# A hybrid decoder layer in fp32: norm spreads with padded parts, later last spreads, and three small reorderings

## The chip, the cores and the metric

The kernel runs on one core of one Trainium2 chip. The metric is the time of one execution on the device, in microseconds. Before the change the median of 3 runs is 1130.23 us (1129.2 to 1131.2).

## The reference

One layer of a decoder is applied to 1056 tokens: a prompt of 1024, and 8 sequences of 4 new tokens each (the decode tokens) that continue from stored keys and values. The width is 1024, everything is fp32, and `_rms(x, g)` is `x / sqrt(mean(x*x) + eps) * g` over the features of a token.

```python
h = _rms(x, n_mix_pre)
z = h @ w_in                       # 1024 -> 512 q | 128 k | 128 v | 512 u
a = attention(q, k, v)             # 8 heads of 64, 2 kv heads, 128 keys incl. self, one sink per head
m = pool_mixer(u)                  # trailing means over 2/4/8/16 tokens minus the token,
                                   # a 128x128 map for each of 4 groups, a scale per channel
mix = concat([a, m]) @ w_out
x = x + _rms(mix, n_mix_post)
f = _rms(x, n_ffn_pre)
f = (silu(f @ w_gate) * (f @ w_up)) @ w_down      # 1024 -> 2816 -> 1024
x = x + _rms(f, n_ffn_post)
x = x + sigmoid(x @ w_ple_gate) * (p @ w_ple)     # p: 256 per token, given
```

The outputs are the new `x` of all tokens, the last 128 keys and values and the last 15 pooling inputs of the prompt, and the same three buffers of the decode sequences, moved on by 4 tokens.

## The kernel before, in words

**Layout.** Features lie on the 128 partitions, tokens along the free dimension. The 1056 tokens are cut into 3 groups of `N` = 352 columns; group 2 holds the last prompt tokens and the decode tokens. A weight is cut into 128x128 blocks, so nearly every matmul has the shape 128x128 by 352 columns.

**Products in threes.** An fp32 value is held as two parts of type fp32r, `hi` and `lo = value - hi`, made by ScalarE and VectorE in `split` (lines 164 and 165). `gemm` (line 291) issues three matmuls for each 128x128 block: hi weight by hi operand, hi weight by lo operand, lo weight by hi operand. An operand of a half of the features is a tile of 4 rows (parts) of 352 fp32 values each, one behind the other, so the k-th part starts 1408k bytes behind the first.

**Weights.** They are streamed from HBM by SyncE's queue through 3 raw buffers (`w_load`), split into 8 buffers of hi and lo (`w_split`), in the order of `plan`, a few tiles ahead of their use. For groups 0 and 1 the wide products use a scheme with 7 quarter products in place of 8 (Strassen's): the sums of weight quarters S1 to S4 are made on GpSimd in `w_sums` (line 1007) and then split; the differences of operands T1 to T4 are made on VectorE (`t_sum` for the FFN, `e_sum` for the last stage). Group 2 uses the direct products.

**A norm's factor** comes from `rstd_steps` (line 313). The squares are summed over the 8 feature blocks into `acc` (128 x 352). Three small matmuls, `acc` in three windows of 128 tokens by a column of ones, sum over the partitions and put tokens on the partitions. ScalarE and VectorE form 1/sqrt, split it in hi and lo, and write each half as a diagonal into `dg` (lines 331 to 344; the tile has the halves behind each other). After a `yield`, two matmuls of 352 columns, a matrix of ones by each half of `dg`, spread the factor over all partitions: this is the spread. There are three norms before the attention (one for each group), two for each group on the way into the FFN (`ffn_steps`, whose second is that of the FFN's input), and one for each group on the FFN's output (`ple_steps`).

**Order of the work.** Most of TensorE's order is that of the program (`pinned`). `order` keeps a VectorE instruction in program order as long as `ordered[0]` is set, that is, up to the first eviction of the opening stage. Everything else is placed by the scheduler of the framework.

- *Opening.* Projections of the pooling inputs `u`, then of k, v and q, for three groups; the pooling mixer between them.
- *Attention.* `dscores` and `scores` make the scores of the decode tokens and of one block of 128 prompt tokens, `softmax` follows on the other engines, then the weights are transposed (`dturned`, `turned`) and applied (`dvalues`, `values`). Blocks go in the order 5, 6, 7, 0, 1, 2, 3, 4, each block's scores ahead of the values of the block before. `filler` puts pieces of the output projection between. The decode values (`dvalues`) are 2 + 16 small matmuls.
- *Output projection and norms.* `turn` and `chain` (lines 891 to 906) are a planner: `chain` adds a generator of steps, `turn(n)` advances a clock by n products of 128x128 by 352 and runs each step that is due. A step says how much VectorE work it has (`load`) and how long to wait; its next due time is the VectorE time so far plus load / `share` plus wait. `share` is 0.6 here, 0.45 in the FFN, 0.1 while the FFN's last group-2 steps run, and 0.7 at the end.
- *The walk.* The FFN's 22 chunks of 128 hidden features go by 11 slabs of 2. `WALK` has 5 slabs (`AHEAD`) for group 2 alone, 6 slabs for all groups, then the first 5 for groups 0 and 1. `gate_up` makes the hidden values, `downs` and `down` the second product of the slab before. `last_down` does this for a group's last slab and gathers squares. When group 2's last slab is done, `chain(ple_steps(2), 19)` starts its norm; `ple_steps(0)` and `ple_steps(1)` start behind the last item (lines 1283 and 1286).
- *End.* `ple_out` handles group 2's eight blocks of 128 features of the last stage directly; `embed_early` makes products `p @ w_ple` ahead of need. `ple_first` then does the first two quarter products of blocks 7, 5, 3 and 1, and `ple_rest(a, b)` the rest of the pairs (1, 0), (3, 2), (5, 4), (7, 6) in that order: T4, S2, S3, S1, S4, each by its partner. `ple_end` forms the sigmoid, multiplies, adds and stores.

The steps of `ple_steps` between small products and spread are these, with the planner's numbers:

```python
yield 6, 14                          # in rstd_steps: load 6, wait 14, then the spread
...
chain(ple_steps(2), 19)              # behind group 2's last slab, share 0.1
chain(ple_steps(0), 24)              # behind the last slab of group 0, share 0.7
chain(ple_steps(1), 54)              # behind the last slab of group 1
```

Of the kernel before, what the change touches and what calls it, by code (L numbers as in the profile page):

```python
# [11 lines left out]
F32R = mybir.dt.float32r  # L12
# [4 lines left out]
P = 128  # L17
# [44 lines left out]
def trunk_kernel(  # L62
# [43 lines left out]
    def nm(s):  # L106
        cnt[0] += 1
        return f"{s}{cnt[0]}"
# [200 lines left out]
    def order(ins):  # L309
        if ordered[0]:  # L310
            tc.keep_in_program_order(ins)

    def rstd_steps(acc):

        n = acc.shape[1]
        at = (0, P, n - P)
        sm = bank()
        for i, lo in enumerate(at):  # L320
            mm(sm[:, i : i + 1], acc[:, lo : lo + P], ones[:, 0:1], start=True, stop=True)
        sd = spool.tile([P, TB], F32, tag="sd", name=nm("sd"))
        se.activation(sd, sm[:, :TB], AF.Sqrt, bias=epst, scale=1.0 / D)
        ve.reciprocal(sd, sd)
        hl = spool.tile([P, 2, TB], F32R, tag="hl", name=nm("hl"))
        ve.tensor_copy(hl[:, 0], sd)
        ve.tensor_tensor(hl[:, 1], sd, hl[:, 0].bitcast(F32), op=ALU.subtract)
        dg = spool.tile([P, 2, n], F32R, tag="dg", name=nm("dg"))
        f = hl.bitcast(F32)
        rest = n - 2 * P  # L330
        dg1 = lambda: ve.tensor_tensor(
            dg[:, :, : 2 * P].rearrange("p h (i k) -> p h i k", k=P),
            ident.unsqueeze(1).unsqueeze(1).to_broadcast([P, 2, 2, P]),
            f[:, :, 0:2].unsqueeze(3).to_broadcast([P, 2, 2, P]),
            op=ALU.mult,
        )
        dg2 = lambda: ve.tensor_tensor(
            dg[:, :, 2 * P :],
            ident[:, P - rest :].unsqueeze(1).to_broadcast([P, 2, rest]),
            f[:, :, 2:3].to_broadcast([P, 2, rest]),  # L340
            op=ALU.mult,
        )
        order(dg1())
        order(dg2())
        yield 6, 14
        ps = bank()
        for h in range(2):
            mm(ps[:, :n], ones_r, dg[:, h], start=h == 0, stop=h == 1)
        return ps[:, :n]
# [4 lines left out]
    def sum_halves(sqs, g):  # L354

        a, b = sqs
        order(ve.tensor_tensor(a, a, b, op=ALU.add))
        ve.tensor_tensor(a[:, 0:2, :], a[:, 0:2, :], a[:, 2:4, :], op=ALU.add)
        acc = acc_tile(g)
        ve.tensor_tensor(acc, a[:, 0, :], a[:, 1, :], op=ALU.add)  # L360
        return acc
# [477 lines left out]
    def filler(n):  # L839
        for _ in range(n):  # L840
            if fill:
                f, *at = fill.pop(0)
                f(*at)
# [5 lines left out]
    filler(2)  # L849
    ptd = dturned(td)  # L850
    filler(1)
    od = bank()
    dvalues(ptd, od)
    put(od, SEQ, NDEC * DSEQ)
# [1 line left out]
    ge.tensor_copy(kse[:, :, : WIN - DSEQ], ckt[:, :, DSEQ:])  # L856
    ge.tensor_copy(kse[:, :, WIN - DSEQ :], kT[:, SEQ:].rearrange("p (b t) -> p b t", t=DSEQ))
    for a, b in zip(blocks, blocks[1:] + [None]):
        t2 = None if b is None else scores(b)
        filler(1)  # L860
        parts = turned(a, t)
        filler(1)
        values(a, parts)
        t = t2
# [49 lines left out]
    def ffn_steps(g):  # L914

        r = yield from rstd_steps(acc[g])
        for yh, xh in zip(ys[g], x1[g]):
            ve.tensor_tensor(yh, yh, bc4(r), op=ALU.mult)
            ve.tensor_tensor(xh, xh, yh, op=ALU.add)
            se.activation(yh, xh, AF.Square)  # L920
            yield 20, 0
        yield 0, 13
        acc2 = sum_halves(ys[g], g)
        yield 20, 6
        r = yield from rstd_steps(acc2)
        for h in range(2):
            nc.sync.dma_start(x1d[g][h], x1[g][h])
            for c in range(4):
                k = 4 * h + c
                ve.scalar_tensor_tensor(  # L930
                    ys[g][h][:, c, :], x1[g][h][:, c, :], gn[:, 2, k : k + 1], r, op0=ALU.mult, op1=ALU.mult
                )
            yield 14, 0
            if (g, h) == (1, 0):
                t_sum("T1")
                yield 20, 0
            else:
                op = f_operand(ys[g][h], g)
                yield 10, 0
                if g == 2:  # L940
                    fs[2].append(op)
                else:
                    f7[f"B{h + 1}{g + 1}"] = op
        if g == 1:
            for name in ("T3", "T2", "T4"):
                t_sum(name)
                yield 20, 0
# [185 lines left out]
    def ple_steps(g):  # L1133

        pl = half(g, F32R, "pl")
        pls[g] = pl[:, 0:2, :], pl[:, 2:4, :]
        for k in range(2):
            pr = tmp(NS[g], "pr")
            nc.sync.dma_start(pr, p[:, k, OFF[g] : OFF[g + 1]])
            split(pl[:, k, :], pl[:, 2 + k, :], pr)  # L1140
        x2s[g] = []
        for h in range(2):
            x2[g][h] = half(g, s="x2")
            nc.sync.dma_start(x2[g][h], x1d[g][h])
        r = yield from rstd_steps(acc3[g])
        behind = tc.keep_in_program_order if g == 2 else lambda ins: ins
        for h in range(2):
            yh, xh = os_[g][h], x2[g][h]
            behind(ve.tensor_tensor(yh, yh, bc4(r), op=ALU.mult))  # L1149
            for c in range(4):  # L1150
                k = 4 * h + c
                behind(
                    ve.scalar_tensor_tensor(  # L1153
                        xh[:, c, :], yh[:, c, :], gn[:, 3, k : k + 1], xh[:, c, :], op0=ALU.mult, op1=ALU.add
                    )
                )
                if g == 2 and c % 2:
                    yield 6, 0
            yield 12 if g == 2 else 24, 0
            if g == 2:  # L1160
                x2s[g].append(f_operand(xh, g))
            elif (g, h) != (1, 0):
                e7[f"B{h + 1}{g + 1}"] = f_operand(xh, g)
            yield 10, 0
        if g == 1:
            for name in ("T1", "T2", "T3", "T4"):
                e_sum(name)
                yield 20, 0
# [85 lines left out]
    def ple_rest(a, b):  # L1254
        wp, w, js = W2[a]
        p1 = p1s[0][:, a // 2, :]

        def add(out, x, ps):
            ve.tensor_tensor(out, x, ps, op=ALU.add)  # L1259

        need(wp)
        a22 = need(w)
        p4 = product(a22, e7["T4"])
        s = need(js)
        add(p1, p1, product(s["S2"], e7["T2"]))
        u3 = tmp(N, "u3")
        add(u3, p1, product(s["S3"], e7["T3"]))
        c21 = tmp(N, "c21")
        add(c21, u3, p4)
        ple_end(c21, wp, b, 0)  # L1270
        p5 = product(s["S1"], e7["T1"])
        add(u3, u3, p5)
        add(p1, p1, p5)
        ple_end(u3, wp, b, 1)
        add(p1, p1, product(s["S4"], e7["B22"]))
        ple_end(p1, wp, a, 1)

    hid[:] = new_hid
# [107 lines left out]
```

## Time and profile before

| what | value |
|---|---|
| median of 3 runs | 1130.23 us |
| profiled execution, its own time | 1130.37 us |
| its span, first to last instruction | 1128.6 us |
| mean granted clock of TensorE | 0.997 |
| TensorE matmul, busy | 1105.4 us, 6997 instructions |
| VectorE, busy | 785.1 us |
| ScalarE, busy | 459.3 us |
| GpSimd, busy | 200.7 us |
| read from HBM, written | 90.55 MB, 10.11 MB |

The profile is of one execution. PE is TensorE's matmul, PEld its weight load, DVE VectorE, ACT ScalarE, POOL GpSimd and SP SyncE. `L126` is the line of the helper that issues nearly all matmuls, so they are told apart by the names of their operands: `mh`, `ml` are the mixers' outputs, `hid` the FFN's hidden values, `fh`, `fl` an operand in hi and lo, `wh`, `wl` a weight, `sh`, `sl` a weight sum, `acc` the summed squares, `dg` the diagonals, `c` a constant. A row of a timeline has start, length, engine, line, operation, output and inputs, shapes and a count; "[a <-X]" behind it says that the engine idled for a us before it, and which instruction ended that. A spread shows as `dg,c` x2, the small products of a norm as `c,acc` with twice the count, as an fp32 matmul leaves two records.

### The profile page before, as it was taken

What the parts mean: (1) busy time and instruction counts of PE and PEld (TensorE: products, weight loads), DVE (VectorE), ACT (ScalarE), POOL (GpSimd) and SP (SyncE); (2) the same over time, 40 slices, a digit from 0 to 9 for tenths busy, and PEclk for the clock granted to TensorE, in tenths of its full rate; (3) what the DMA queues carried; (4) which work ended last, traced back from release to release, by engine and by line L of the source; (5) the groups of instructions that cost most, each with busy time, mean ns of one, the idle gap of its engine ahead of it and who ended that gap; (6) DMA issues with size and microseconds to landing.
All of it is one profiled execution on the core that took longest, in us unless ns stands there. A gap on an engine that the chain in (4) does not pass through costs nothing.

```text
span 1128.6 us, 17518 instructions
## 1 busy us (share of the span) xinstructions
PE 1105.4 (98%) x6997; PEld 1085.6 (96%) x6997; DVE 785.1 (70%) x1296; ACT 459.3 (41%) x823; POOL 200.7 (18%) x169
## 2 busy tenths in 40 slices
PE   8999999999999999999999999999999999999986
PEld 8999978899999999999999999999999999999986
DVE  6766368876979955355465555548887877789887
ACT  8322367665645433331222213123424334356442
POOL 0044022100000221021111102111141132100242
PEclk9999999999999999999999999999999999999999
DMA  8121310442643212021120202113212212246141
GB/s 286 57 69 42 111 50 23 178 178 89 219 137 133 87 45 87 19 75 38 38 76 12 82 20 75 38 38 119 82 53 94 71 61 94 94 145 216 62 151 64
DMA packets 35986, 101.79 MB, mean 90 GB/s; under 512 B 4260, under 2 KB 14916, under 8 KB 35904
## 3 DMA queue, kind: packets, MB, share of 16 engines
q1 hardware_dynamic: 34576, 98.90, 25.8%
q10 hardware_dynamic: 1328, 1.77, 0.5%
q8 instruction: 55, 0.90, 0.3%
q14 instruction: 27, 0.22, 0.1%
HBM read 90.55 MB, written 10.11 MB: 89 GB/s over the span
## 4 chain that ended last, share of the span: by engine, by line
PE 87%; DVE 4%; ACT 3%; issue 2%; POOL 1%; DMA 1%; POOLq 0%; ACTq 0%; SPq 0%; DVEq 0%
PE b L126 87%; POOL wr L1007 1%; DMA xr<-in_x_dram 1%; PE b L120 1%; ACT h L392 1%; ACT wh L164 0%; DVE sg L1220 0%; DVE yo L1222 0%; DVE o L1130 0%; ACT sh L164 0%; ACT a L662 0%; DMA c<-in_gains_dram 0%; DVE o L1149 0%; DMA wr<-in_w_in_dram 0%; DVE x L1153 0%
## 5 line engine op out<-in xcount | busy, mean ns | idle before, releaser
L126 PE MATMUL b<-hid,wh 128*128 128x352 f32 x1056 | 254.3, 322 | 2.6 <-DVE o L1149 2.1
L164 ACT CAST wh<-wr 128x1024 fp32r<-128x1024 f32 (+1 forms) x135 | 138.6, 1029 | 255.0 <-PE b L126 203.3
L126 PE MATMUL b<-fh,wh 128*128 128x352 f32 x712 | 230.1, 323 | 0.0
L126 PE MATMUL b<-fh,wl 128*128 128x352 f32 x712 | 230.0, 323 | 0.0
L126 PE MATMUL b<-fl,wh 128*128 128x352 f32 x712 | 228.6, 321 | 0.0
L1007 POOL TENSOR_TENSOR wr<-wr 128x512 f32<-128x512 f32 x52 | 72.0, 1385 | 744.8 <-DVE wl L165 459.0
L165 DVE TENSOR_TENSOR wl<-wr,wh 128x1024 fp32r<-128x1024 f32 (+1 forms) x135 | 165.4, 1228 | 45.2 <-ACT wh L164 44.7
L126 PEld LDWEIGHTS b<-hid,wh 128*128 128x128 f32 x1056 | 184.6, 188 | 3.3 <-issue 2.4
L126 PE MATMUL b<-hid,wl 128*128 128x352 f32 x528 | 170.4, 323 | 0.0
L126 PE MATMUL b<-fh,sl 128*128 128x352 f32 x416 | 134.6, 324 | 4.8 <-DVE sl L165 4.8
L1104 DVE TENSOR_TENSOR o<-o,b 128x352 f32<-128x352 f32 x240 | 115.1, 515 | 30.5 <-PE b L126 30.2
L126 PE MATMUL b<-fh,sh 128*128 128x352 f32 x416 | 134.7, 324 | 0.5 <-DVE p L1259 0.5
L126 PEld LDWEIGHTS b<-fl,wh 128*128 128x128 f32 x712 | 134.9, 189 | 0.0
L126 PE MATMUL b<-fl,sh 128*128 128x352 f32 x416 | 133.5, 321 | 0.0
L126 PEld LDWEIGHTS b<-fh,wl 128*128 128x128 f32 x712 | 133.4, 187 | 0.0
L126 PEld LDWEIGHTS b<-fh,wh 128*128 128x128 f32 x712 | 133.4, 187 | 0.0
L165 DVE TENSOR_TENSOR sl<-wr,sh 128x1024 fp32r<-128x1024 f32 x52 | 63.6, 1222 | 82.0 <-ACT sh L164 82.0
L164 ACT CAST sh<-wr 128x1024 fp32r<-128x1024 f32 x52 | 53.9, 1047 | 145.3 <-POOL wr L1007 102.3
L126 PE MATMUL b<-h,wh 128*128 128x352 f32 x480 | 104.8, 323 | 1.2 <-ACT h L392 1.0
L126 PEld LDWEIGHTS b<-hid,wl 128*128 128x128 f32 x528 | 98.9, 187 | 0.0
L126 PEld LDWEIGHTS b<-fh,sl 128*128 128x128 f32 x416 | 77.9, 187 | 6.3 <-DVE sl L165 6.3
L126 PEld LDWEIGHTS b<-h,wh 128*128 128x128 f32 x480 | 81.5, 188 | 2.3 <-ACT h L392 1.3
(186 smaller groups left out, 1690.4 us busy)
## 6 DMA issues: line engine op xcount, KB each, us to landing
wr<-in_w_gu_dram SPq DMA_DIRECT2D x64, 512.0 KB, 3.3
wr<-in_w_dn_dram SPq DMA_DIRECT2D x32, 512.0 KB, 3.6
wr<-in_w_pg_dram SPq DMA_DIRECT2D x18, 512.0 KB, 3.5
x<-in_x_dram SPq DMA_DIRECT2D x6, 704.0 KB, 9.2
x1d<-x SPq DMA_DIRECT2D x6, 704.0 KB, 3.5
x<-x1d SPq DMA_DIRECT2D x6, 704.0 KB, 6.8
out_y_dram<-yo SPq DMA_DIRECT2D x24, 176.0 KB, 1.8
wr<-in_w_out_b_dram SPq DMA_DIRECT2D x8, 512.0 KB, 3.5
```

What stands on the lines that cost most here:

```text
L120: ins = te.transpose(out, src, ident)
L126: ins = te.matmul(*args, **kw)
L164: fix(se.copy(hi, src))
L165: fix(ve.tensor_tensor(lo, src, hi.bitcast(F32), op=ALU.subtract))
L392: fix(se.activation(hi[:, c, :], t[:, c, :], AF.Identity, scale=gc))
L1007: ge.tensor_tensor(out, a, b, op=op)
L1104: ve.tensor_tensor(o, o, v, op=ALU.add)
```

## The change

1. *Padding.* `dg` is allocated with 384 columns per half and used up to 352, so that the second half starts 1536 instead of 1408 bytes behind the first. This is so for every norm.
2. *Even small products.* With `even` set, `rstd_steps` issues a fourth small product, a repetition of the third into a column that nobody reads. `even` is set for the norm of the FFN's input of group 1 alone, the last norm in the program before those of `ple_steps`.
3. *Last spreads.* The wait between small products and spread becomes an argument; it is 28 instead of 14 for the three norms in `ple_steps`.
4. *Decode values.* In the attention, the scores of block 6 are issued ahead of the decode values and no longer behind them.
5. *S4.* In `ple_rest`, the product of S4 and B22 is issued behind that of S2 and T2, for all pairs but the last, and its sum goes onto p1 behind the S3 product; before, it was the last of the pair.
6. *First add of squares.* `sum_halves` keeps its first add in program order only for group 1. As `order` works only in the opening stage, and group 2's is made after that, this concerns group 0's first add in the opening.

```diff
-    def rstd_steps(acc):
+    def rstd_steps(acc, wait=14, even=False):
         n = acc.shape[1]
         at = (0, P, n - P)
         sm = bank()
-        for i, lo in enumerate(at):
+        for i, lo in enumerate(at + at[2:] * even):
             mm(sm[:, i : i + 1], acc[:, lo : lo + P], ones[:, 0:1], start=True, stop=True)
...
-        dg = spool.tile([P, 2, n], F32R, tag="dg", name=nm("dg"))
+        dg = spool.tile([P, 2, 3 * P], F32R, tag="dg", name=nm("dg"))[:, :, :n]
...
-        yield 6, 14
+        yield 6, wait
         ps = bank()
...
     def sum_halves(sqs, g):
         a, b = sqs
-        order(ve.tensor_tensor(a, a, b, op=ALU.add))
+        add = ve.tensor_tensor(a, a, b, op=ALU.add)
+        if g == 1:
+            order(add)
...
     filler(1)
+    t2 = scores(blocks[1])
     od = bank()
     dvalues(ptd, od)
...
     for a, b in zip(blocks, blocks[1:] + [None]):
-        t2 = None if b is None else scores(b)
+        t2 = None if b is None else t2 if a == blocks[0] else scores(b)
...
-        r = yield from rstd_steps(acc2)
+        r = yield from rstd_steps(acc2, even=g == 1)
...
-        r = yield from rstd_steps(acc3[g])
+        r = yield from rstd_steps(acc3[g], 28)
...
         add(p1, p1, product(s["S2"], e7["T2"]))
+        early_s4 = b < KC - 2
+        if early_s4:
+            s4 = product(s["S4"], e7["B22"])
         u3 = tmp(N, "u3")
         add(u3, p1, product(s["S3"], e7["T3"]))
+        if early_s4:
+            add(p1, p1, s4)
         c21 = tmp(N, "c21")
...
         ple_end(u3, wp, b, 1)
-        add(p1, p1, product(s["S4"], e7["B22"]))
+        if not early_s4:
+            add(p1, p1, product(s["S4"], e7["B22"]))
         ple_end(p1, wp, a, 1)
```

## The prediction

> **What bounds the kernel now.** I read the page first, then the timeline of TensorE for its idle stretches, then counts in long windows.
>
> ```profile
> span 1128.6 us, 17518 instructions
> PE 1105.4 (98%) x6997; PEld 1085.6 (96%) x6997; DVE 785.1 (70%) x1296; ACT 459.3 (41%) x823; POOL 200.7 (18%) x169
> ```
>
> TensorE is the bound almost everywhere, so two things can move the end: its idle stretches, and the time from one matmul's start to the next. For the second I put two stretches without idle time beside each other; the columns are window, length, TensorE's busy time and instructions, then the other engines, the granted clock, the DMA share and GB/s.
>
> ```profile
> 400.00:790.00 390.00, 390.00 (x2422) 390.00 (x2421) 214.63 (x357) 109.25 (x169) 63.94 (x48) 1.00 0.17 55
> 882.00:1002.00 120.00, 120.00 (x757) 120.00 (x756) 92.34 (x147) 48.63 (x69) 27.61 (x20) 1.00 0.28 90
> ```
>
> Both are full of the same 128x128 by 352 products at full clock. A matmul takes 0.32, so those that reach over an edge add 0.32 to the stretch: 390.32/2422 = 161.1 ns each in the walk, 120.32/757 = 158.9 ns later. The same product has two paces, 2.2 ns apart. Where they change shows in the timeline of TensorE (start, length, operation): `c,acc` are the small products of a norm, `dg,c` its spread of two parts.
>
> ```profile
> 228.02 0.41 PE L126 MATMUL b<-mh,wh 128*128 128x352 f32 x1
> 231.97 0.51 PE L126 MATMUL b<-dg,c 128*128 128x352 f32 x2
> 232.32 0.32 PE L126 MATMUL b<-mh,wh 128*128 128x352 f32 x1
> ...
> 257.11 0.72 PE L126 MATMUL b<-c,acc 128*128 128x1 f32 x6
> 257.69 0.41 PE L126 MATMUL b<-mh,wh 128*128 128x352 f32 x1
> ...
> 261.59 0.49 PE L126 MATMUL b<-dg,c 128*128 128x352 f32 x2
> 261.92 0.32 PE L126 MATMUL b<-mh,wh 128*128 128x352 f32 x1
> ...
> 277.38 1.39 PE L126 MATMUL b<-c,acc 128*128 128x1 f32 x12
> 278.64 0.41 PE L126 MATMUL b<-fh,wh 128*128 128x352 f32 x1
> ...
> 347.75 0.49 PE L126 MATMUL b<-dg,c 128*128 128x352 f32 x2
> ...
> 795.64 0.72 PE L126 MATMUL b<-c,acc 128*128 128x1 f32 x6
> 796.22 0.41 PE L126 MATMUL b<-fh,sh 128*128 128x352 f32 x1
> ...
> 809.66 0.49 PE L126 MATMUL b<-dg,c 128*128 128x352 f32 x2
> ```
>
> By the code 24 products lie between 228.02 and 231.97 (less the first one's 0.08: 161 ns), 156 between 232.32 and 257.11 (158.9), 24 between 257.69 and 261.59 (159.0), 96 between 261.92 and 277.38 (161.0), 84 between 796.22 and 809.66 (159.0). So the pace is a state: it lasts for as long as products come in their usual threes, and it flips at a spread (232 to fast, 261.6 and 809.7 to slow) or at small products (795.6 to fast; 257 leaves it fast, 277 slow). After 347.75 nothing but threes comes until 795.6: whatever pace the last spread leaves holds for the whole walk, and it left the slow one.
>
> **The change part by part**, against this execution's 1130.37 (span 1128.6 and 1.8 around it); the runs' median, 1130.23, is the same to 0.01%.
>
> **Pace: padded parts, four small products.** A row of 352 values is 1408 bytes, so the k-th part of any operand starts at 1408k: the even parts on a multiple of 256, the odd ones halfway. The usual threes alternate three even, three odd; the spread is one even, one odd. Padded to 384 (1536 bytes), it is two even. The trace has no such spread. Its price lies between no effect and a whole fast walk: 795.64 less 347.75 and the spread is 447.5 us, 2778 products at 161.1; at 158.9 they take 6.1 us less. Taking the spread for ordinary products, and for each next start the one that the trace has after the nearest position of the starts with the same parities, I get what happened for one even and one odd part (slow) and, for two even ones, mostly the fast pace out of a slow one and a middle pace (about 160 ns, half the gain, 3.1) out of a fast one. That is an estimate, with little to hold it beyond two steps. I take -6.1. The fourth product changes which pace meets the last spread: six more small records took (278.64 - 277.38) - (257.69 - 257.11) = 0.68, so two more cost +0.2. All later norms have padded spreads too: the 120 us stretch above, and all of 825 to 1003 us, is fast now and could turn slow: 178/0.159 = 1120 products, +2.5 at most; I take 0, as the walk meets it differently anyhow.
> The Trainium skill (TensorE: Matmul & The Clock Gate, "Back-to-back issue gap") has the time from start to start depend on the number of columns alone, some 149 ns for 352. By it neither padding nor a fourth product could change the pace, and this term would be 0; the two windows above, the same shape at one clock, speak against it, but none shows what padding does.
>
> **Decode values behind block 6's scores.**
>
> ```profile
> 136.30 2.12 PE L126 MATMUL b<-a,a 64*128 64x32 f32 x20
> 138.35 0.43 PE L126 MATMUL b<-mh,wh 128*128 128x352 f32 x1
> ...
> 144.48 0.32 PE L126 MATMUL b<-mh,wl 128*128 128x352 f32 x1
> 146.90 4.91 PE L126 MATMUL b<-a,a 32*64 32x128 f32 x52 [2.10 <-ACT y L802]
> 151.74 0.57 PE L126 MATMUL b<-mh,wh 128*128 128x352 f32 x1
> ```
> ```profile
> 146.35 0.41 DVE L777 COPY a<-b 32x256 f32<-32x256 f32 x1
> ```
> ```profile
> 145.00:148.60 3.60, 1.70 (x38) 1.53 (x40) 0.82 (x4) 2.02 (x10) 2.66 (x3) 1.00 0.10 40
> 148.60:152.00 3.40, 3.40 (x17) 2.33 (x15) 1.06 (x3) 0.91 (x4) 0.53 (x2) 0.51 0.38 154
> ```
>
> TensorE could go on at 144.64 (144.48 + 0.16) and waits to 146.90. The page names a copy on ACT; VectorE's copy of the turned decode weights ends at the same time (146.76), and these products read it. Then come 36 records of decode values and 16 of block 6's scores; the clock falls to 0.51 from 148.6, and the scores run at half speed. At full clock 20 records with block 5's scores took 2.05 (136.30 to 138.35). With the scores first: 144.64 + 2.0 = 146.6, a rest of 0.3 to 146.9 for the copy, decode values as before (52 records end at 151.74; the 36 at about 148.3, since the scores start the slow stretch), next product at 148.3 instead of 151.74, and that product's own 0.25 of slow clock is gone too: -3.7. Scores and values issue no DMA; block 6's copies and softmax get onto ACT and VectorE earlier, ahead of the values' copies. Bounds: -3.9, and -2.0 if the clock still falls (it would then halve 3.4 us of full products).
> The Trainium skill (the same page, "What's actually happening") has the clock fall after an idle window of about 3.4 us. The wait here was 2.3, and the waits of 2.1 below cost no clock: by this rule the wait is not the cause, the many small products may be, and they stay.
>
> **Last spreads 14 products on.** By the code's own reckoning (each step is due a load divided by a share after the last, plus the wait, at the next turn), group 2's spread moves from 84 to 96 products behind its small ones, and its VectorE steps with it.
>
> ```profile
> 824.76 0.43 PE L126 MATMUL b<-hid,wh 128*128 128x352 f32 x1 [0.44 <-DVE hid L165]
> ...
> 873.38 0.56 PE L126 MATMUL b<-hid,wh 128*128 128x352 f32 x2 [2.11 <-DVE o L1149]
> ```
> ```profile
> 870.48 1.23 DVE L165 TENSOR_TENSOR sl<-wr,sh 128x1024 fp32r<-128x1024 f32 x1 [3.73 <-ACT sh L164]
> 871.62 1.61 DVE L1149 TENSOR_TENSOR o<-o,b 128x1408 f32<-128x1408 f32 x1
> ```
>
> TensorE stands 2.1 us for a bank while VectorE does a split and the norm's multiply (L1149), which stand ahead of the evictions. Two products' groups later the multiply stands behind some of them. Both waits gone: -2.6; the 1.6 us multiply met elsewhere: up to +1.6. I take -1.1, about half the larger wait, as the split stays where it is.
>
> Group 0's spread:
>
> ```profile
> 1007.50 0.32 PE L126 MATMUL b<-hid,wl 128*128 128x352 f32 x1
> 1009.92 0.58 PE L126 MATMUL b<-dg,c 128*128 128x352 f32 x2 [2.10 <-DVE dg L337]
> ```
> ```profile
> 1003.00:1066.00 63.00, 60.90 (x383) 60.61 (x382) 59.92 (x83) 38.06 (x53) 1.54 (x2) 1.00 0.43 148
> ```
>
> By the same reckoning it moves 30 products on (due 36.6 behind its small ones, next turn at 54 instead of 24), past 1012.4; its operand is there by 1009.9, so the 2.3 us wait is gone. But VectorE is busy 59.92 of 63 us here, and the end game hangs on it:
>
> ```profile
> 1063.48 0.68 DVE L165 TENSOR_TENSOR w<-wr,w 128x512 fp32r<-128x512 f32 x1
> ```
> ```profile
> 1064.38 1.30 POOL L1007 TENSOR_TENSOR wr<-wr 128x512 f32<-128x512 f32 x1 [90.11 <-DVE w L165]
> ...
> 1088.58 1.30 POOL L1007 TENSOR_TENSOR wr<-wr 128x512 f32<-128x512 f32 x1 [5.89 <-DVE w L165]
> ...
> 1101.48 1.51 POOL L1007 TENSOR_TENSOR wr<-wr 128x512 f32<-128x512 f32 x1 [7.02 <-DVE w L165]
> ```
>
> POOL's sums of the last weights start when VectorE has split a tile (1063.48), and then go round every 12 to 13 us with a load, a split and the next sum, whatever TensorE does. So of the 2.3 us only what lets VectorE reach 1063.48 sooner survives. Group 1's spread stays at its turn, the differences T1 to T4 come 36 products later in the program, behind that split rather than ahead of it: up to two steps of 1.6 us earlier for POOL, or idle VectorE time for want of work. I take -1.2, bounds -3.2 and +5.8 (36 products of 161 ns).
>
> **S4 moved.**
>
> ```profile
> 1087.95 0.43 PE L126 MATMUL b<-fh,sl 128*128 128x352 f32 x1 [0.66 <-DVE sl L165]
> ...
> 1100.83 0.43 PE L126 MATMUL b<-fh,sl 128*128 128x352 f32 x1 [1.77 <-DVE sl L165]
> ```
>
> S3 waits for the second split in pairs (3, 2) and (5, 4); S4 needs only the first, and its 12 products (1.9 us) fill both waits, 2.4 together. But TensorE then arrives that much earlier at the next pair's first split, which hangs on POOL's round above. No DMA moves: p1's output still leaves last. I take -0.3, bounds -2.4 and 0.
>
> **Start.** Group 0's first add of squares loses its place in VectorE's order; VectorE's queue decides a single wait:
>
> ```profile
> PE b L126 <- DVE acc L360: 1.0, 1, 1.0
> ```
>
> 0, bounds 0 and +0.6 (one more operation ahead of it, as long as one eviction).
>
> Sum: -6.1 + 0.2 - 3.7 - 1.1 - 1.2 - 0.3 = -12.2; 1130.4 - 12.2 = 1118.2.
>
> **The rivals.**
> *Middle pace.* The last spread is met in the fast state and leaves 160 ns: -3.1 instead of -6.1, 1121.2. For it: the same estimate gives this for half the possible entries. Against: the fourth product shifts the entry.
> *The pace stays.* The state flips for another reason than the parts' places, or padding doesn't reach it: the walk at 161.1, 1124.3. For it: 277 left the pace slow with twelve small records. Against: 261.6 and 809.7, where an even and an odd part ended a fast stretch twice alike.
> *The clock still falls* behind the decode values: 1118.2 + 1.7 = 1119.9. For it: waits of 2.1 at 873 and 1009.9 kept full clock, so idleness alone isn't it. Against: block 5's scores with decode scores at 134 to 138 kept it too.
> *Late spreads starve the end (slower).* VectorE, with nothing to do until group 0's spread lands 30 products later, brings T1 to T4 and POOL's first sum 5.8 us later, and group 2's multiply stands in front of another wait (+1.6). With a walk that stays slow that is -3.7 + 0.2 + 1.6 + 5.8 = +3.9: 1134.3. It decides once the delay of the end exceeds the 3.5 that the decode part saves. For it: 59.92 of 63 leaves no slack. Against: VectorE has 60 us of other work there.
>
> **How the numbers follow.** Forecast 0.50, middle pace 0.21, pace stays 0.15, clock falls 0.07, starved end 0.07. A measurement here tells 0.2% (2.3 us) from no change. Faster: all of the first, second and fourth, and two thirds of the third; the rest of it and a little of the last are within: 0.88 / 0.07 / 0.05. Without the unlikely ends the forecast's own range is 1115 to 1121. It reaches up over the middle and the unchanged pace, 1126, and down to 1113.5, where the waits at 824 and 873 go altogether and POOL starts two steps earlier.
>
> **What would show it.** Right: a window inside the walk at 158.9 ns a product; no TensorE idle time near 145 and clock 1.00 to 152; block 6's scores ahead of the decode values; no wait for `dg` behind the last walk item; POOL's first sum no later than 1064.4 less what was gained before. Wrong: 161 ns in the walk, a stretch at 161 between 825 and 1003, a new wait for `fh` or `fl` at T4's product, or longer waits for the first split of each pair in place of the second.

## The result, and the profile after

The changed kernel takes 1119.11 us (median of 4 runs, 1117.57 to 1120.09), the kernel before in the same session 1129.72; the ratio is 0.9906 (95% interval 0.9886 to 0.9925). Run again later on another occasion, the same kernel gave 1117.87 us and 0.9883 (0.9868 to 0.9898) against 1131.45. The profiled execution is at 1118.45, its span at 1116.7. The forecast was 1118.2.

The page of the changed kernel begins so:

```profile
span 1116.7 us, 17519 instructions
...
PE 1098.3 (98%) x6999; PEld 1080.0 (97%) x6999; DVE 778.4 (70%) x1296; ACT 458.8 (41%) x823; POOL 201.2 (18%) x169
```

The span is 11.9 us shorter. To see where, I put the start of the same 352-column product in the two profiles side by side (counted from the first product; the products of the spreads are left out of the count):

| product | before | after | difference | gained since the row above |
|---|---|---|---|---|
| 96, behind the opening's first 96 products | 24.25 | 23.79 | -0.46 | -0.5 |
| 800, behind the decode values | 153.27 | 149.31 | -3.96 | -3.5 |
| 1800, early in the walk | 352.91 | 348.35 | -4.56 | -0.6 |
| 4535, last item but one ahead of 795 us | 793.55 | 782.91 | -10.64 | -6.1 |
| 4735, behind the first wait at group 2's spread | 827.41 | 817.99 | -9.42 | +1.2 |
| 5010, behind the second | 873.38 | 862.12 | -11.26 | -1.8 |
| 5735, ahead of group 0's spread | 988.66 | 979.11 | -9.55 | +1.7 |
| 5850, behind it | 1010.34 | 998.32 | -12.02 | -2.5 |
| 6200, start of the last stage's pairs | 1067.49 | 1055.47 | -12.02 | 0.0 |
| the last | 1121.76 | 1109.44 | -12.32 | -0.3 |

**The walk.** Windows of the changed kernel (window, length, TensorE's busy time and instructions, the other engines, granted clock, DMA share, GB/s):

```profile
258.00:273.00 15.00, 15.00 (x97) 15.00 (x96) 13.65 (x18) 9.54 (x14) 0.00 (x0) 1.00 0.35 111
400.00:790.00 390.00, 390.00 (x2458) 390.00 (x2458) 216.26 (x362) 111.89 (x172) 68.38 (x52) 1.00 0.17 54
906.00:1002.00 96.00, 96.00 (x599) 96.00 (x598) 75.08 (x131) 41.55 (x62) 16.75 (x12) 1.00 0.33 109
```

In the same 390 us of the walk there are 2458 products, not 2422: 390.32/2458 = 158.8 ns each. The clock is 1.00 in both. From 906 to 1002 us it is the other way round: 96.32/599 = 160.8, where the kernel before had 158.9. The timeline of TensorE shows where the pace of the walk is set:

```profile
257.56 0.48 PE L126 MATMUL b<-dg,c 128*128 128x352 f32 x2
...
333.68 0.94 PE L126 MATMUL b<-c,acc 128*128 128x1 f32 x8
...
343.27 0.48 PE L126 MATMUL b<-dg,c 128*128 128x352 f32 x2
...
784.98 0.72 PE L126 MATMUL b<-c,acc 128*128 128x1 f32 x6
...
800.91 0.48 PE L126 MATMUL b<-dg,c 128*128 128x352 f32 x2
```

The spread at 343.27 is the last before 784.98, as the one at 347.75 was. It was met in the slow pace in both kernels: the 52 products between its small products and it go at 161.2 ns. The spread at 257.56 was met in the fast pace, and the products behind it keep that pace: 97 in the 15 us, where 161 ns would show 95 or 96. In the kernel before the pace turned slow at this spread.

**The decode values.** TensorE's timeline and windows:

```profile
144.25 2.00 PE L126 MATMUL b<-a,a 64*128 64x256 f32 x16
146.50 1.48 PE L126 MATMUL b<-a,a 32*64 32x128 f32 x36 [0.25 <-ACT y L804]
```
```profile
145.00:148.60 3.60, 3.35 (x52) 2.71 (x49) 2.41 (x8) 2.79 (x12) 2.77 (x4) 1.00 0.08 32
148.60:152.00 3.40, 3.40 (x26) 3.38 (x25) 2.75 (x11) 2.48 (x14) 0.13 (x1) 1.00 0.01 2
```

The scores now fill the wait (2.00 us at full clock, a rest of 0.25), and the clock does not fall.

**The last spreads.** TensorE no longer stands for `dg` at group 0's spread. Of the two waits near group 2's spread, the second is nearly gone and the first has grown; a third has come:

```profile
814.93 1.00 PE L126 MATMUL b<-hid,wh 128*128 128x352 f32 x2 [1.62 <-ACT hid L164]
...
862.12 0.59 PE L126 MATMUL b<-hid,wh 128*128 128x352 f32 x2 [0.27 <-DVE o L1107]
...
905.70 0.59 PE L126 MATMUL b<-hid,wh 128*128 128x352 f32 x2 [0.28 <-DVE o L1107]
...
1003.15 0.48 PE L126 MATMUL b<-dg,c 128*128 128x352 f32 x2
```

The first waits for ScalarE's cast of a hidden value. ScalarE's timeline, the kernel before first and then the changed one:

```profile
820.14 0.49 ACT L164 CAST hid<-u 128x352 fp32r<-128x352 f32 x1 [1.72 <-DVE u L1085]
824.35 1.05 ACT L164 CAST sh<-wr 128x1024 fp32r<-128x1024 f32 x1 [3.73 <-POOL wr L1007]
```
```profile
813.45 1.04 ACT L164 CAST sh<-wr 128x1024 fp32r<-128x1024 f32 x1 [3.68 <-POOL wr L1010]
814.40 0.48 ACT L164 CAST hid<-u 128x352 fp32r<-128x352 f32 x1
```

The two casts have changed places: the hidden value now stands behind the cast of a weight sum, which waits 3.68 us for GpSimd.

**The end.** GpSimd's first sum of the first, second and last of its four last rounds, and TensorE's waits for the splits in the pairs:

```profile
1053.39 1.29 POOL L1010 TENSOR_TENSOR wr<-wr 128x512 f32<-128x512 f32 x1 [88.92 <-DVE w L165]
...
1065.53 1.55 POOL L1010 TENSOR_TENSOR wr<-wr 128x512 f32<-128x512 f32 x1 [5.46 <-DMA wr<-in_w_pg_dram]
...
1089.62 1.51 POOL L1010 TENSOR_TENSOR wr<-wr 128x512 f32<-128x512 f32 x1 [5.86 <-DVE w L165]
```
```profile
1074.09 0.43 PE L126 MATMUL b<-fh,sl 128*128 128x352 f32 x1 [0.67 <-DVE sl L165]
...
1084.89 0.43 PE L126 MATMUL b<-fh,sh 128*128 128x352 f32 x1 [1.31 <-ACT sh L164]
...
1086.98 0.43 PE L126 MATMUL b<-fh,sl 128*128 128x352 f32 x1 [1.51 <-DVE sl L165]
```

GpSimd starts 10.99 us earlier than before (1064.38), about a microsecond less than TensorE had gained by product 6200, and TensorE has a new wait of 0.89 in front of the first weight sum (at 1062.88). From the first round's start to the fourth's it is 36.23 us, where it was 37.10. The two waits at 1084.89 and 1086.98 are for the two halves, `sh` and `sl`, of one tile's split, the first of the pair.

### The profile page after: what moved, and what is told of

Read it like the earlier page. It is cut to its first block, busy times and chain, and to the rows that moved or that the text cites. A ratio compares the mean times of both kernels' runs of the same rounds, so it can differ in the third digit from the quotient of the medians.

```text
span 1116.7 us, 17519 instructions
## 1 busy us (share of the span) xinstructions
PE 1098.3 (98%) x6999; PEld 1080.0 (97%) x6999; DVE 778.4 (70%) x1296; ACT 458.8 (41%) x823; POOL 201.2 (18%) x169
## 4 chain that ended last, share of the span: by engine, by line
PE 82%; DVE 6%; POOL 3%; ACT 3%; issue 2%; DMA 2%; ACTq 0%; SPq 0%; POOLq 0%; DVEq 0%
PE b L126 81%; POOL wr L1010 3%; DVE wl L165 1%; DVE sl L165 1%; ACT sh L164 1%; DMA xr<-in_x_dram 1%; PE b L120 1%; DVE o L1133 1%; ACT h L394 1%; DVE sg L1223 1%; DVE yo L1225 1%; DMA wr<-in_w_pg_dram 0%; ACT wh L164 0%; DMA wr<-in_w_gu_dram 0%; ACT a L664 0%
## 5 line engine op out<-in xcount | busy, mean ns | idle before, releaser
L1010 POOL TENSOR_TENSOR wr<-wr 128x512 f32<-128x512 f32 x52 | 75.0, 1442 | 736.1 <-DVE wl L165 453.4
L126 PEld LDWEIGHTS b<-fh,sh 128*128 128x128 f32 x416 | 78.0, 188 | 4.8 <-ACT sh L164 2.0
```

What stands on the lines that cost most here:

```text
L126: ins = te.matmul(*args, **kw)
L1010: ge.tensor_tensor(out, a, b, op=op)
```

## The experiments

Times stand against the kernel before in the same session, whose median was 1131.4 to 1131.7 us in all of them; the changed kernel had two sessions of its own (1119.11 and 1117.87), so single microseconds are read from the profiles.

### What sets the pace of the walk

**The distance of the halves**, in the changed kernel:

```diff
-        dg = spool.tile([P, 2, 3 * P], F32R, tag="dg", name=nm("dg"))[:, :, :n]
+        dg = spool.tile([P, 2, 416], F32R, tag="dg", name=nm("dg"))[:, :, :n]
```

> The changed kernel with one number altered: a half of dg takes 416 columns and not 384, so the second half starts 1664 bytes behind the first, which is again halfway between multiples of 256, as the 1408 of the kernel before. Theory of the place (the spread flips the pace by whether its second part stands at an even or an odd multiple of 128 bytes): the spread behind the four small products leaves the slow pace, the walk goes at 161 ns a product, 6.1 us longer, and the time is about 1125 us (1124 to 1126.5). Rival, padding as such (any shift of the tiles in memory, or the fourth small product, or the earlier entry into the walk, sets the pace): the walk stays at 158.9 ns and the time at 1119 us.

1125.68 us (ratio 0.9952, 0.9938 to 0.9966). The walk of this kernel:

```profile
400.00:790.00 390.00, 390.00 (x2423) 390.00 (x2422) 213.46 (x354) 109.15 (x169) 64.00 (x48) 1.00 0.16 54
```

390.32/2423 = 161.1 ns. More padding, and the gain of the walk is gone: padding as such falls, the place of the second half decides.

**Both halves at odd places**, in the changed kernel:

```diff
-... name=nm("dg"))[:, :, :n]
+... name=nm("dg"))[:, :, 32 : 32 + n]
```

> The changed kernel with dg's columns 32 to 383 used in place of 0 to 351: both halves then start at odd multiples of 128 bytes, where the changed kernel has both at even ones and the kernel before one of each. Theory of like places (only halves of unlike places leave the slow pace): the walk is not at 161 ns, but at 158.9 (1119.1) or, as the replay of the old trace's starts has it, at 160 (1122.2). Rival (a multiple of 256 for both is what counts): the walk at 161 ns, 1125.2.

1119.64 us (0.9893, 0.9862 to 0.9925), and the walk is fast:

```profile
400.00:790.00 390.00, 390.00 (x2458) 390.00 (x2457) 216.23 (x362) 111.82 (x172) 67.66 (x51) 1.00 0.17 55
```

So a multiple of 256 is not what counts for the walk: at the last spread two halves at like places leave the fast pace, two at unlike places the slow one. Places are counted from the start of the tile, whose own address no profile shows. The middle pace, which the replay of the old starts gave, did not come in the walk.

**Three small products in place of four**, in the changed kernel:

```diff
-        r = yield from rstd_steps(acc2, even=g == 1)
+        r = yield from rstd_steps(acc2)
```

> The changed kernel with three small products in place of four ahead of group 1's last spread in front of the walk. Theory A (the padded spread alone sets the pace, since the three small products leave the slow pace here as those at 322 us did): the walk stays at 158.9 ns, 1119 us less 0.2. Theory B (three small products leave the fast pace, and a padded spread met in it leaves the middle one): the walk at 160 ns, 3.1 us longer, 1122 us. Theory C (the number of small records decides): the walk at 161 ns, 6.1 longer, 1125 us.

1118.6 us (0.9888, 0.9857 to 0.992), and 2458 products in the 390 us once more:

```profile
400.00:790.00 390.00, 390.00 (x2458) 390.00 (x2458) 216.26 (x362) 111.82 (x172) 67.95 (x51) 1.00 0.16 54
```

Theory A. The other side of it is **the fourth small product alone**, in the kernel before:

```diff
-        for i, lo in enumerate(at):
+        for i, lo in enumerate(at + at[2:] * even):
...
-        r = yield from rstd_steps(acc2)
+        r = yield from rstd_steps(acc2, even=g == 1)
```

> The kernel before with the fourth small product ahead of group 1's last spread and nothing else, dg at 352 columns. Theory of the places (a spread of unlike halves leaves the slow pace, however it is met): the walk stays at 161 ns a product, 1130 us. Rival (the fourth product shifts the entry so that the spread leaves another pace): the walk at 158.9 or 160 ns, 1124 or 1127 us.

1132.38 us (one run):

```profile
400.00:790.00 390.00, 390.00 (x2423) 390.00 (x2422) 215.16 (x359) 109.37 (x170) 63.96 (x48) 1.00 0.16 54
```

The walk stays slow. The fourth product neither is needed nor does anything by itself.

**Padding alone**, in the kernel before:

```diff
-        dg = spool.tile([P, 2, n], F32R, tag="dg", name=nm("dg"))
+        dg = spool.tile([P, 2, 3 * P], F32R, tag="dg", name=nm("dg"))[:, :, :n]
```

> The kernel before with nothing but the padding of dg to 384 columns. Theory A (padding alone sets the pace): the walk at 158.9 ns, 6.1 us less than before, some 1123.7 us; with the middle pace, 3.1 less, 1126.7. Theory C (the fourth small product is needed): the walk stays at 161 ns and the time within 1 us of the kernel before, 1129.7. If the pace behind 825 us turns slow, up to 2.5 us come on top.

1125.23 us (0.9948, 0.9928 to 0.9967), 6.2 less than before, with a fast walk in the profiled execution:

```profile
400.00:790.00 390.00, 390.00 (x2458) 390.00 (x2457) 217.17 (x363) 112.55 (x173) 64.93 (x49) 1.00 0.17 56
```

Its ten runs lie between 1121.4 and 1128.4, wider than those of the changed kernel, and the profiled one is among the shortest (1122.04); what the longer ones did was not seen.

**How far the rule of like places goes.** In all 14 profiles it holds at the last spread ahead of the walk, which was met in the slow pace each time, at the spread near 258 us, at group 2's near 800 and at the very last one. It does not hold everywhere. Behind the spread near 228 us, with the halves at like places, the changed kernel's first profile, its second one and the run with three small products show this:

```profile
229.00:252.00 23.00, 23.00 (x147) 23.00 (x146) 17.18 (x23) 12.84 (x22) 0.00 (x0) 1.00 0.30 109
229.00:252.00 23.00, 23.00 (x145) 23.00 (x144) 17.03 (x23) 12.66 (x22) 0.00 (x0) 1.00 0.29 109
229.00:252.00 23.00, 23.00 (x146) 23.00 (x145) 17.66 (x24) 13.13 (x22) 0.00 (x0) 1.00 0.29 110
```

By the starts these are 158.9, 161.1 and 160.0 ns: the first two come from one program, and the third is the middle pace, which exists. Two spreads back to back near 283 us leave 161.1 ns in every profile but that of both halves at odd places, which has 158.9. What sets these is open.

### The decode values

```diff
     filler(1)
+    t2 = scores(blocks[1])
     od = bank()
     dvalues(ptd, od)
...
-        t2 = None if b is None else scores(b)
+        t2 = None if b is None else t2 if a == blocks[0] else scores(b)
```

> The kernel before with block 6's scores ahead of the decode values and nothing else. Theory: TensorE's wait of 2.26 us at 144.6 us goes and the clock stays at 1.00 up to 152 us; 3.5 us less than before, 1126.2 us (1125.5 to 1127), and all later paces as before, the walk at 161 ns. Rival (the clock falls behind the decode values all the same): 2.0 less, 1127.7. Rival (the gain is lost later, because the attention waits for softmax): within 1 us of 1129.7.

1127.28 us (0.9968, 0.9953 to 0.9984). TensorE's timeline of this kernel has the same two rows as the changed one:

```profile
144.68 2.00 PE L126 MATMUL b<-a,a 64*128 64x256 f32 x16
146.94 1.48 PE L126 MATMUL b<-a,a 32*64 32x128 f32 x36 [0.26 <-ACT y L802]
```

A ratio of 0.9968 is 3.6 us (1.8 to 5.3 by its interval), in line with the 3.5 of the table: the gain is kept to the end, and the walk stays slow here (2423 products in the 390 us).

### The last spreads

**Group 2 at 14 again**, in the changed kernel:

```diff
-        r = yield from rstd_steps(acc3[g], 28)
+        r = yield from rstd_steps(acc3[g], 14 if g == 2 else 28)
```

> The changed kernel with the wait of 14 back for group 2's spread (28 stays for groups 0 and 1). Theory of the exchange (the later spread only moved the multiply of L1152 from one wait to another): the wait behind the walk's end, 1.9 us for the hi part of hid, shrinks to 0.6, the one some 46 us later grows from 0.3 to 2.1, and the time is within 0.7 us of the changed kernel's 1119.1; if the stretch behind it, now at 161 ns a product for 98 us, turns fast, up to 1.8 less. Rival (the prediction's term of -1.1 for the later spread is right): 1.1 longer, 1120.2.

1117.37 us (0.9877, 0.9847 to 0.9908). Both waits are back, at 0.57 and 1.58 where the kernel before had 0.44 and 2.11:

```profile
814.39 0.43 PE L126 MATMUL b<-hid,wh 128*128 128x352 f32 x1 [0.57 <-DVE hid L165]
...
862.48 0.56 PE L126 MATMUL b<-hid,wh 128*128 128x352 f32 x2 [1.58 <-DVE o L1152]
```

0.57 + 1.58 = 2.15 with the earlier spread, 1.62 + 0.27 + 0.28 = 2.17 with the later: an exchange. The forecast's -1.1 for this step falls. The five other profiles with 14 beside the kernel before have 1.3 to 1.8 in the two waits together, so the 2.11 was a long one; the seven with 28 have 1.8 to 2.2. In two of the seven the clock fell behind the first wait as well (0.73 from 820 to 826 us in the run with 416 columns, 0.66 from 815 to 820 with three small products).

**Group 0 at 14 again**, in the changed kernel:

```diff
-        r = yield from rstd_steps(acc3[g], 28)
+        r = yield from rstd_steps(acc3[g], 14 if g == 0 else 28)
```

> The changed kernel with the wait of 14 back for group 0's spread alone. In any case TensorE waits some 2.3 us for dg again behind the walk's last item. Theory A (POOL's rounds carry half of it to the end, as forecast): 1.2 us longer, 1120.3. Theory B (the whole wait reaches the end): 2.3 to 2.6 longer, 1121.6. Theory C (POOL's first sum is as early as before, so nothing reaches the end): 1119.1.

1121.5 us (0.9917, 0.9889 to 0.9944), 2.4 to 3.6 above the changed kernel. TensorE's wait, a window behind it, and GpSimd's first sum of the end:

```profile
1000.03 0.65 PE L126 MATMUL b<-dg,c 128*128 128x352 f32 x2 [2.10 <-DVE dg L337]
```
```profile
1000.40:1004.00 3.60, 3.60 (x15) 3.60 (x14) 3.60 (x7) 0.95 (x2) 0.00 (x0) 0.53 0.00 0
```
```profile
1055.77 1.29 POOL L1010 TENSOR_TENSOR wr<-wr 128x512 f32<-128x512 f32 x1 [91.40 <-DVE w L165]
```

By its number this is Theory B, but part of it is the clock. It fell behind the wait (0.53 for 3.6 us), which it had not done behind the same wait in the kernel before:

```profile
1010.00:1014.00 4.00, 4.00 (x25) 4.00 (x26) 4.00 (x7) 0.95 (x2) 0.00 (x0) 1.00 0.00 0
```

Counted from product 5735, which precedes the wait, product 5880 starts 28.04 us later here, 26.49 in the kernel before and 24.36 in the changed one: 2.1 for the wait, 1.55 for the clock. GpSimd's first sum starts 77.01 behind product 5735 here (1055.77 - 978.76), 75.72 in the kernel before and 74.28 in the changed one. Padding alone and the four small products alone, at full clock, have 75.46 and 75.81; scores first, with the clock at 0.53 behind the wait, has 77.29. So at full clock the earlier spread costs GpSimd's first sum 1.2 to 1.5 us, near the forecast's half, while TensorE loses the whole wait. The fourth sum is later by all of it again: 112.82 behind product 5735 in the kernel before, 110.51 in the changed one. Why the rounds between are longer with the earlier spread was not looked into.

### S4 moved

```diff
-        early_s4 = b < KC - 2
+        early_s4 = False
```

> The changed kernel with S4's product back at the end of every pair. Forecast: 0.3 us longer, 1119.4, because the waits of the next pair's first split grow by what those of the second shrink. Rival (the 12 products fill waits that nothing takes back): up to 2.4 longer, 1121.5.

1118.18 us (0.9882, 0.9852 to 0.9912). TensorE's waits in the pairs of this kernel:

```profile
1075.01 0.43 PE L126 MATMUL b<-fh,sl 128*128 128x352 f32 x1 [0.67 <-DVE sl L165]
...
1085.53 0.43 PE L126 MATMUL b<-fh,sh 128*128 128x352 f32 x1 [0.93 <-ACT sh L164]
...
1086.79 0.43 PE L126 MATMUL b<-fh,sl 128*128 128x352 f32 x1 [0.67 <-DVE sl L165]
1089.35 0.43 PE L126 MATMUL b<-fh,sl 128*128 128x352 f32 x1 [0.38 <-DVE sl L165]
```

Neither expectation: it is no longer. These four waits are 2.65, the three of the changed kernel 3.49. The wait for `sh` is there with S4 last too (0.93); moving S4 took the 0.38 of the second split and made the two waits for the first split longer, 1.31 + 1.51 in place of 0.93 + 0.67. The times alone (1118.18 against 1119.11 and 1117.87) do not tell, but the starts do: from product 6200 to the last it takes 53.4 to 55.0 us in the six profiles with S4 moved and 28 for group 0, and 53.1 and 53.3 in the two with S4 last (this one and the one with both steps undone). In three of the six the clock fell behind these waits (0.50 to 0.73 for 6 us), in the two it did not.

### The changed kernel again, and two versions beside it

**The same kernel** (no edit):

> The changed kernel once more, beside the next ones on one chip, so that differences of a microsecond can be read. Expected: the walk at 158.9 ns a product as in its first profile, 1119 us (1117.5 to 1120.5), and, if the slow stretch from 905 to 1003 us hangs on a wait of 0.45 us, that stretch again at 161 ns.

1117.87 us. Its windows:

```profile
906.00:1002.00 96.00, 96.00 (x606) 95.85 (x605) 76.20 (x132) 41.55 (x62) 16.64 (x12) 1.00 0.33 109
...
1086.00:1092.00 6.00, 6.00 (x21) 6.00 (x22) 5.86 (x11) 0.57 (x2) 3.24 (x3) 0.50 0.48 147
```

The walk is as before (2459 products in the 390 us). The slow stretch from 906 to 1002 us is not: 96.32/606 = 158.9. So the pace in that stretch differs between executions of one program, as it does behind the spread near 228 us, while the last spread left the same pace in both. The wait of 0.28 in front of the stretch is 0.15 here by the starts; but two other runs (three small products, group 0 at 14) have 0.25 there and stay at the fast pace. And here the clock fell to 0.50 from 1086 to 1092 us, where the first profile of this kernel has 1.00.

**Group 2 at 14 and S4 last together:**

> The changed kernel with group 2's spread at 14 again and S4's product at the end of each pair again; padding, four small products, scores first and 28 for groups 0 and 1 stay. If the two undone steps cost 1.7 and 0 to 0.9 us, as their own runs suggest: 1116.5 us, 1 to 3 us below the changed kernel. Rival (those differences were scatter): within 0.7 us of it.

1116.64 us (0.9868, 0.9852 to 0.9885), 1.2 below the changed kernel in the same session, with overlapping intervals. Undoing the two steps costs nothing; that it gains is likely and not settled by the times.

**Two of the four sums on VectorE in the last stage**, in that kernel (`i` numbers the four sums from 0):

```diff
-            ge.tensor_tensor(out, a, b, op=op)
+            (ve if tail[0] and i in (1, 3) else ge).tensor_tensor(out, a, b, op=op)
...
     early = {}
+    tail[0] = True
```

> The kernel with group 2's spread at 14 and S4 last, and in the last stage the second and fourth of the four weight sums on VectorE and not on GpSimd. If GpSimd's rounds bound the end, each round is some 2.4 us shorter, TensorE's waits in the last pairs (6.5 us in the changed kernel) shrink by 2 to 5 us, and the time is 1112 to 1114.5 us. Rival (VectorE, busy most of that time, is the bound, and its two more operations of some 0.6 us each stand in front of splits and evictions): the waits stay or grow, 1116 to 1119 us.

1112.91 us (0.9845, 0.9822 to 0.9867), the shortest of all; its four runs lie between 1111.52 and 1117.16, and the profiled one is the shortest. GpSimd's first sum of the first and the last round with the last round's second one, and TensorE's waits in the pairs:

```profile
1051.63 1.30 POOL L1012 TENSOR_TENSOR wr<-wr 128x512 f32<-128x512 f32 x1 [88.47 <-DVE w L165]
...
1085.27 1.50 POOL L1012 TENSOR_TENSOR wr<-wr 128x512 f32<-128x512 f32 x1 [5.18 <-DVE w L165]
...
1089.57 1.51 POOL L1012 TENSOR_TENSOR wr<-wr,wr 128x512 f32<-128x512 f32 x1 [2.79 <-DVE wr L1012]
```
```profile
1070.42 0.43 PE L126 MATMUL b<-fh,sl 128*128 128x352 f32 x1 [0.35 <-DVE sl L165]
...
1082.25 0.50 PE L126 MATMUL b<-fh,sh 128*128 128x352 f32 x1 [2.28 <-ACT sh L164]
1083.51 0.66 PE L126 MATMUL b<-fh,sl 128*128 128x352 f32 x1 [0.46 <-DVE sl L165]
```

From the first round's start to the fourth's it takes 33.64 us, and 1088.66 - 1052.96 = 35.70 in the kernel without this edit. The rounds are shorter by 0.7 each and not by 2.4, since GpSimd's second sum now waits up to 2.79 us for VectorE to do its own. Against the kernel without this edit, beside it, the median is 3.7 less and the span of the profile 5.7 (1109.7 against 1115.4). By the starts of the same products 1.3 of the 5.7 are there before the last stage (1023.25 against 1021.92 us; 0.5 of them from product 96 on, so not from the edit), 1.8 come in the last stage (the last product starts at 1108.30 against 1105.19), and 2.6 behind the last product. There VectorE begins seven operations after the last product's start without this edit and two with it. So GpSimd's rounds bound a part of the end; why VectorE is less behind, with two operations more to do in each round, was not looked into.

## Why the prediction was right, step by step

The time and the way were right: -12.2 forecast, -11.9 in the span. The terms, one by one:

- **Pace of the walk, -6.1: right.** The table has -6.1, and the distance of 416 columns takes the gain away again. The pace as a state that the last spread leaves, and the halves' places as what flips it there, both held. The estimate behind it was half right. For a spread of two even parts met in the slow pace it gave mostly the fast one, and so it came: the last spread was met in the slow pace in all 14 profiles. For one met in the fast pace it gave the middle one; at 257.56 it leaves the fast one. The condition of the rival of the middle pace, a last spread met in the fast state, never arose, with three small products or four; the rival of a pace that stays falls by the count. The prediction called this an estimate with little to hold it, and there is some luck in it: behind the spread near 228 us halves at like places do not leave the fast pace each time.
- **Fourth small product, +0.2.** The count of its records is as forecast (8 against 6, 0.22 us longer); as a means to shift the entry it does nothing for the walk, with padding or without (the latter in one run).
- **The Trainium skill's rule** (TensorE: Matmul & The Clock Gate, "Back-to-back issue gap"), by which the columns alone set the spacing and this term would be 0: the runs decide against it, with 161.1 and 158.8 ns for the same shape at clock 1.00, and a layout that switches between them. The 149 ns are worked out from the section's formula for an isolated matmul, of which it says that it gives too much for a stream at many columns; here it gives too little.
- **Decode values, -3.7: right** (-3.5), with the rest of 0.25 forecast as 0.3, and the clock kept. The rival of the falling clock falls here.
- **Group 2's spread, -1.1: wrong.** The second wait went as argued, from 2.11 to 0.27, as the multiply now stands behind the evictions. What failed is "Both waits gone": the first one grew from 0.44 to 1.62, by way of ScalarE's order, which the prediction had not looked at, and 0.28 came new, so that 1.46 of the 1.84 were lost again. Against group 2 at 14 in the changed kernel nothing is left of the gain.
- **Group 0's spread, -1.2: right in kind, too small.** GpSimd's first sum gained 1.2 to 1.5 at full clock, about as forecast. The failing sentence is that of the 2.3 us "only what lets VectorE reach 1063.48 sooner survives", taken as a cap on the end: TensorE kept 2.1 to the start of the pairs' products, and GpSimd's fourth sum gained 2.3, since its rounds became shorter. Up to 3.6 in the run with 14 has 1.55 of fallen clock in it.
- **S4, -0.3: wrong in sign.** By the starts moving it back saves 0.2 to 1.9 us between product 6200 and the last one. That the wait goes to the first split was right: 2.82 there with S4 moved, 1.60 with S4 last.
- **Start, 0.** Its -0.5 is scatter: the small products of group 0's first norm start at 23.20 in the changed kernel, at 23.57 and 23.83 in two others with that edit, and at 23.52 and 23.73 in two without.
- **Not forecast:** the slow stretch from 905 us, +1.3 in that profile (98 us at 161 in place of 158.9), taken at 0 with bounds up to +2.5; it came behind a wait, not behind a padded spread, and is not there in the second profile of the same program. And the products from 6000 to 6200 take 31.78 us where they took 32.22, -0.4: they stand behind the very last spread, whose halves are at like places now.

Of the signs of being wrong that the prediction names, two appeared, a stretch at 161 ns between 825 and 1003 us and a longer wait for a first split. That the sum came within 0.3 us is luck: group 0's spread, the faster pace in the last stage and half a microsecond of scatter at the start made up for what group 2's spread and S4 gave less and for the slow stretch. The slower rival, a starved end, has nothing for it: GpSimd's first sum came 10.99 us earlier, not later.

## What to carry to other kernels

When TensorE is busy all the time, count its instructions in long windows: two counts for the same shape at the same clock are a lever no idle time shows, and here 128 bytes of layout, 32 columns of padding behind an operand of 352, decided 6 us. A step that is moved to clear one wait must be followed through the queues of every engine that serves it; ScalarE's order of two casts took back what VectorE's order gave. And where an engine off the path starts a chain of rounds, ask what its start follows: here it moved by 10.99 of the 12.02 us that the bound engine had gained. A run that puts a wait back can also bring a fallen clock with it, 1.55 us here, which has to be taken out before the wait is priced.

## What was not expected of the hardware

- **A lasting pace, set by the places of two operands.** In all 14 profiles the walk goes at 161.1 ns when the halves of `dg` start at unlike multiples of 128 bytes (the kernel before, 416 columns, scores first, four small products) and at 158.8 to 158.9 when they are alike (the ten others, both at even or both at odd). Three distances were tried: 1408, 1536 and 1664 bytes. Elsewhere a third pace, 160.0 ns, lasts for some 150 products, and one program shows 158.9 and 161.1 at the same place in two executions. How two products set the pace of 2778 that follow is not shown.
- **The clock falls behind waits much shorter than the time that it then stays low, and not every time.** Group 0's wait of 2.1 us left 1.00 in three profiles (the kernel before, padding alone, four small products alone) and 0.53 for 3.6 us in two (group 0 at 14, scores first). Two waits of 1.31 and 1.51 in the pairs left 1.00 in the changed kernel's first profile; 1.06 and 1.50 at the same place left 0.50 for 6 us in its second. The Trainium skill (TensorE: Matmul & The Clock Gate, "What's actually happening") calls the window in which activity is judged free-running; that the same wait has both outcomes agrees with it, and no run here shows where a window began. The waits themselves were below the 3.4 us that the section gives for one idle window, so by that figure alone none of them should have cost clock; the measurement decides.
